# The second product of the stick-breaking scores over 128 rows instead of 64

## The chip, the cores and the metric

The kernel runs on one core of a Trainium2 chip. What counts is the device time of one execution in microseconds (us). It is taken as the median of several runs; one further execution was recorded by the hardware profiler, and all rows below come from that one.

## What is computed

A trunk of two layers over 512 tokens of width 1024, in float32. In each layer three kinds of attention work on the same normalised input, and their results are projected, gated and summed; a SwiGLU feed-forward part (FFN) follows. The change is in the third kind, the stick-breaking attention with 8 heads of 64 features. Its scores are plain products of queries and keys:

```python
def stick_breaking_attention(q, k, v):
    scale = q.shape[-1] ** -0.5
    ...
        z = jnp.einsum('bhqd,bhkd->bhqk', qb, k, preferred_element_type=jnp.float32) * scale
        log_beta = jax.nn.log_sigmoid(z)
        log_keep = jnp.where(mask, jax.nn.log_sigmoid(-z), 0.0)
        suffix = lax.cumsum(log_keep, axis=3, reverse=True) - log_keep
        a = jnp.where(mask, jnp.exp(log_beta + suffix), 0.0)
        return jnp.einsum('bhqk,bhkd->bhqd', a.astype(v.dtype), v)
```

## The kernel before

**Products in two parts.** TensorE is used with operands in the format fp32r. To keep the accuracy of float32, an operand is held as a hi part (rounded to fp32r) and a lo part (what the rounding left). A product of weights and activations is then three products, hi·hi, hi·lo and lo·hi (`mm3`, L199 to L201). The tiles are 128 partitions by 512 columns, one column for each token.

**Order of the work.** TensorE issues in exactly the order in which the program is written; the other engines follow an order that a scheduler makes at build time. Each layer's attention runs in windows 1 to 12, one for each pair of heads: four pairs of forgetting attention (tiles `sf`), four of latent attention (`sm`), four of stick-breaking (`ss`, windows 9 to 12, heads 16 to 23). Within a window the steps of large products (`proj`, `gate`, `o`, three matmuls to a step) stand between the small products of the current head and of the head before it. `SLOTS["s"]` gives that order for a stick-breaking head: the scores of query block 3, then 2, 1, 0, with transposes (L457, `pts`) and products with the values (L468 to L471) of the head before in between.

**The scores of a stick-breaking head.** A pair of heads shares a projection tile: rows 0 to 63 are the first head's features, rows 64 to 127 the second's. `head_q` writes for each head a tile `qa` with the queries' hi in its own 64 rows and their lo in the other 64. `head_k` writes `ka` with the keys' hi in both halves (ScalarE writes one half, L614; a DMA from the GpSimd queue copies it to the other, L616) and the keys' lo (VectorE, L615). So one product over 128 rows (L735) gives hi·hi + lo·hi, and a second one (L736) must add hi(q)·lo(k). Before the change the keys' lo of both heads share one tile `kb`, each head in its own half, and L736 runs over that half alone: 64 rows. For query block i both products have (i + 1)·128 columns, so the widths 512, 384, 256 and 128 occur once for each head. After the scores VectorE adds the mask to the last 128 columns (L423), ScalarE makes two sigmoids (`lefts` and `ps`, L101), VectorE scans and multiplies (L433, L434), and the next head's slot transposes the result.

The forgetting heads have the same pair of products: L675 over 128 rows, and L676 over 66 rows, since two further rows with sums of the gates stand below the keys' lo.

**Rooms.** PSUM tiles of the large products (`mm`) have three buffers; `proj` of a pair's keys stays in one until L615 has read it. The tile `vt` (L399) carries a pair's values from PSUM to their transposes (L404); it has one buffer. `rope_queries` (L696 to L706) makes the rotated queries of four latent heads with VectorE and GpSimd in a tile `qr`. In L199, L735 and so on, L is the line of the kernel before; the changed kernel's lines lie four further on from L734 of it (L739 and L740 are the two products there).

Of the kernel before, what the change touches and what calls it, by code (L numbers as in the profile page):

```python
# [17 lines left out]
P = 128  # L18
D = 1024
S = 512  # L20
# [12 lines left out]
# columns of the constants  # L33
C_INV, C_SGN, C_N = 0, 1, 2
# columns of the small vectors of a layer
# [4 lines left out]
# the blocks of queries whose weights ScalarE normalises  # L40
SCALE_ACT = {"f": (3,), "m": (2, 3)}
# between steps of the products: scores of a head (c), and transposes and products of the head before (p)
# [8 lines left out]
# products of constants that keep TensorE's clock up at the start  # L51
WARM = (24, 12)
# steps of products before each norm of the latents
WAIT = (8, 3, 8, 4)
# the chunk after which the rope tables are made
ROPE_AT = 4
# the chunk of the first products of the FFN after which the second half's norm comes
SS_AT = 3
# how far the work of attention goes before other work in the schedule, and steps by which the weights' division waits
HP, LAG = 30, 1  # L60

# 2*pi in parts of 8 bits, so that a product with a whole number below 2**16 is exact
# [4 lines left out]
def tile_hybrid_trunk(ctx: ExitStack, tc: tile.TileContext, xT, cvec, pos, cst, cmask, vec, gfin,  # L67
# [19 lines left out]
    # TensorE issues in the order written here; the other engines as the scheduler finds best  # L87
    ctx.enter_context(tc.manual_schedule(engines={pe.engine}))

    # ScalarE's functions, in phases of one table set each  # L90
# [15 lines left out]
    def windows(l):  # L106
        """Units of matrix products to run beside the attention of a pair of heads."""
        fox = [[("proj", l, 3 * p + i) for i in range(3)] for p in range(4)]
        sb = [[("proj", l, 12 + 3 * p + i) for i in range(3)] for p in range(4)]
        mla = [[("uqr", l, p // 2)] * (p % 2 == 0) + [("uq", l, p), ("ukv", l, p)] for p in range(4)]  # L110
        mg = [("merge", l, b, m) for b in range(3) for m in range(KC)]
        w = fox + [mla[0], mla[1] + [sb[0][0]], mla[2] + [sb[0][1]], mla[3] + [sb[1][0]], [sb[0][2], sb[1][1]]]
        w.append([mg[0], sb[1][2], mg[1], mg[2]])
        for p in range(2, 4):
            w.append([u for i in range(3) for u in (mg[3 * p - 3 + i], sb[p][i])])
        return w + [mg[9:14], mg[14:16], mg[16:]]
# [42 lines left out]
    def divide(want, after=None):  # L159
        """hi and lo of the weights before the want-th; after: what goes before them on ScalarE and VectorE"""  # L160
        while len(splits) < min(want, len(LOADS)):
            j = len(splits)
            fetch(j + 1)
            c = LOADS[j][2]
            p_, tag = wp, ""
            if fourth[0]:
                fourth[1] += 1
                if fourth[1] % 4 == 1:
                    p_, tag = fourth[0], "x"
            wh = p_.tile([P, D], F32R, tag="wh" + tag, name="wh")  # L170
            ins = [act.copy(wh[:, :c], raws[j][:, :c]).ins]  # L171
            wl = p_.tile([P, D], F32R, tag="wl" + tag, name="wl")
            ins.append(dve.tensor_sub(wl[:, :c], raws[j][:, :c], wh[:, :c].bitcast(F32)).ins)  # L173
            for i, a in zip(ins, after or ()):
                tc.add_manual_dep(i, a.name, order, reason="more urgent")
            splits.append((wh, wl))

    def W(unit, n=1, raw=3, ready=2, lag=0):
        """The next n weights, of that unit on, as (hi, lo); later ones are on their way."""
        i = at[0]  # L180
        if fourth[0]:
            raw, ready = 4, 3
        assert LOADS[i][0] == unit, (LOADS[i][0], unit)
        at[0] = i + n
        divide(i + n)

        def ahead():
            divide(i + max(n, ready + 1))
            fetch(i + max(n, raw + 1))

        if lag:
            later(lag, ahead)
        else:
            ahead()
        return splits[i] if n == 1 else splits[i : i + n]

# [6 lines left out]
    def gemm(o, wt, acts, m=P, start=True, stop=True, c0=0, cols=FULL):  # L203
        """o += W^T a over the chunks of acts, in steps; wt = (hi, lo) holds them m columns each from c0 on."""
        wh, wl = wt
        n = len(acts)
        for k, (ah, al) in enumerate(acts):
            cs = slice(c0 + k * m, c0 + (k + 1) * m)
            mm3(o, wh[:, cs], wl[:, cs], ah[:, cols], al[:, cols], start and k == 0, stop and k == n - 1)
            if k < n - 1:  # L210
                yield
# [12 lines left out]
    def steps(n):  # L224
        """n steps of the products in the queue"""
# [24 lines left out]
    H = S // 2  # L250

    class Norm:
        """1/sqrt(mean of squares over the features) of half the tokens, in every partition."""
# [77 lines left out]
    make_identity(nc, identf)  # L331
    # additive masks of the diagonal block: a query sees keys <= it, and keys < it
# [9 lines left out]
    # rope tables, rows alike in each 32: cos, and -sin | +sin  # L342
# [9 lines left out]
    # sin: +-r; cos: sin(pi/2 - |r|)  # L352
# [10 lines left out]
    def ada(l, i, c, wt=None, on_pool=False, after=None):  # L363
        """Column c of part i of the modulation."""
# [12 lines left out]
        if i in (1, 4):  # L377
            # g * (1 + scale)
# [16 lines left out]
    # ================= layers =================  # L395
    def values(ap, psv, name, got):
        """[2 heads' features, tokens] in PSUM -> [keys, block, head, hi | lo of the features]."""
# [14 lines left out]
    class Head:  # L412
# [4 lines left out]
        def S(self, i):  # L417
# [8 lines left out]
            if self.kind == "s":  # L426
                # sigmoid(z) of the key times the product of sigmoid(-z) over the later keys
# [20 lines left out]
        def T(self, js):  # L448
            """The weights of key blocks js, keys on the partitions, as hi and lo."""
# [12 lines left out]
        def PV(self, j):  # L462
            """[64 features, queries] += values^T weights^T; rows 0-63: hi of the values, rows 64-127: lo."""
# [12 lines left out]
    def slot(cur, prev, n):  # L476
        """The scores of a head and the rest of the head before it, between n steps of the queue."""
# [13 lines left out]
    for l in range(L):  # L491
# [32 lines left out]
        if l == 0:  # L524
# [4 lines left out]
            def warm(n):  # L529
                """Products of constants while there is nothing else: TensorE's clock falls when it idles."""  # L530
# [5 lines left out]
            # room that has no other use yet  # L536
# [65 lines left out]
        # of a head: qa = its queries' hi and lo, ka = its keys' hi twice; kb = its keys' lo  # L602
# [80 lines left out]
        def latent_keys(pr):  # L683
            """The rows that are alike in all heads"""
# [11 lines left out]
        def rope_queries(quad, ts):  # L696
            qr = rp.tile([P, S], F32, tag="qr", name="qr")
# [26 lines left out]
        def stick_tiles(pr, i, t):  # L724
            ts = sbt[pr % 2]
            qa, ka, kb = ts[0:2], ts[2:4], ts[4]
            if i == 0:
                head_q(qa, t)
            elif i == 1:
                head_k(ka, (kb, kb), t, False)  # L730
                vals["s", pr] = []
                for a in range(2):
                    def scores(t, i, n, qa=qa[a], ka=ka[a], kb=kb, me=slice(a * 64, a * 64 + 64)):
                        qs_ = slice(i * P, (i + 1) * P)  # L734
                        pe.matmul(t[:, :n], qa[:, qs_], ka[:, :n], start=True, stop=False)  # L735
                        pe.matmul(t[:, :n], qa[me, qs_], kb[me, :n], start=False, stop=True)  # L736
# [5 lines left out]
        def merge(u, b, m):  # L742
            """merged[m] += sigmoid(gate) * (y_b w_o)"""
# [32 lines left out]
        # the first pair's projections, with the forget gates and the norms of the latents  # L776
        enqueue(0)
        steps(1)
        with scoped(f"fg{l}", "right") as lp:
            # log of the forget gates: min(z, 0) - ln(1 + exp(-|z|)); its sums, negated  # L780
# [31 lines left out]
        sbt = [[sp.tile([P, S], F32R, name=f"sb{j}{i}") for i in range(5)] for j in range(2)]  # L812
# [151 lines left out]
def _inputs(x, c, positions, g_mix, w_ada, b_ada, w_in, b_fox_f, g_mla_q, w_mla_uq, g_mla_kv,  # L964
            w_mla_ukv, w_o_fox, w_o_mla, w_o_sb, w_out, g_ffn, w_ffn_gate, w_ffn_up, w_ffn_down, g_final):
    """The arrays of the launch: the inputs, laid out for it."""
# [5 lines left out]
    def tiles(w):  # L972
        # [L, K, N] -> [L, N / 128, 128 rows of a chunk, chunks, 128]
        l, k, n = w.shape
        return w.reshape(l, k // P, P, n // P, P).transpose(0, 3, 2, 1, 4)
# [4 lines left out]
    def col(v):  # L980
        # [L, n * 128] -> [128, L, n]
# [6 lines left out]
    def qkv(w):  # L988
        # q, k, v tiles of a pair of heads, pair after pair
# [9 lines left out]
    # l kc p quad head part 32 -> l quad p part kc head 32  # L999
    uqr = uqr.reshape(L, 3, P, 2, 4, 2, 32).transpose(0, 3, 2, 5, 1, 4, 6).reshape(L, 2, P, 768)  # L1000
    ukv = np.asarray(w_mla_ukv).reshape(L, 2, P, 4, 2, 2, 64)  # l kc p pair head k|v 64
    ukv = ukv.transpose(0, 3, 2, 5, 1, 4, 6).reshape(L, 4, P, 512)

    wo = np.stack([np.asarray(w_o_fox), np.asarray(w_o_mla), np.asarray(w_o_sb)], axis=1)  # L 3 512 1024
# [15 lines left out]
    # row i: queries of the first half of block i; keys of its second half  # L1020
# [25 lines left out]
# 10000 ** (-i / 16) in float32  # L1046
# [25 lines left out]
```

## Time and profile before

| | |
|---|---|
| runs | 1897.41, 1897.56, 1901.94 us; median 1897.56 us |
| profiled execution | span of 1895.3 us from its first to its last instruction |
| TensorE (PE) | busy 1857.2 us, 98% of the span, 8956 matmuls |
| weight loads (PEld) | busy 1515.1 us, 80%, beside the matmuls |
| VectorE (DVE) | busy 1169.2 us, 62% |
| ScalarE (ACT) | busy 852.1 us, 45% |
| GpSimd (POOL) | busy 141.8 us, 7% |
| granted TensorE clock | 0.995 of full speed, mean over the span |

The profiled execution has no other time on record than its span; the median of the runs is 2.3 us above it. A matmul is two instructions in the trace: a load of the stationary operand (PEld, LDWEIGHTS) and the product that streams the moving operand (PE, MATMUL). Matmuls are pipelined: a record goes on until the result has come out, so records overlap, and the cost of one is read from start to start, not from its duration. "Idle before" with "issue" is time in which an engine waited for nothing that the profile shows.

### The profile page before, as it was taken

The page shows a single profiled execution, that of the slowest core. Times are in us where ns is not written, and L with a number is a line of the kernel's source. Part 1 is how long each engine was busy: PE and PEld are TensorE (multiplying, and loading weights), DVE is VectorE, ACT ScalarE, POOL GpSimd, SP SyncE. Part 2 cuts the span into 40 slices and gives each one's busy share as a digit, 9 for nine tenths or more (in the row PEclk, how much of TensorE's full clock was granted, in tenths as well). Part 3 has the DMA queues.
Part 4 walks back from the last instruction along what each step waited for, and adds up shares of the span by engine and source line. Part 5 has one row for each costly group of instructions (what it writes and reads, how often), then busy time and mean ns, then how long its engine had stood idle before and what let it go on. Part 6 is the DMA issues. An engine that isn't in the chain of part 4 may idle for free.

```text
span 1895.3 us, 24083 instructions
## 1 busy us (share of the span) xinstructions
PE 1857.2 (98%) x8956; PEld 1515.1 (80%) x8956; DVE 1169.2 (62%) x2043; ACT 852.1 (45%) x1543; POOL 141.8 (7%) x260
## 2 busy tenths in 40 slices
PE   6999999999999999999999999999999999999998
PEld 4788787777889888778897887777788888888887
DVE  8888887677756655554558898666664463333333
ACT  4767874443334322232237688544433342232321
POOL 4122100001000000000002121000110000000000
PEclk8999999999999999999999999999999999999999
DMA  7423323333642655555633222122142222223231
GB/s 276 141 73 81 82 79 117 102 110 131 208 150 70 211 177 184 171 184 194 197 107 101 66 68 85 66 84 83 68 145 99 97 100 100 95 95 98 92 92 53
DMA packets 76741, 224.22 MB, mean 118 GB/s; under 512 B 10768, under 2 KB 13968, under 8 KB 76624
## 3 DMA queue, kind: packets, MB, share of 16 engines
q1 hardware_dynamic: 69136, 213.30, 33.8%
q0 software_dynamic: 7488, 9.38, 2.5%
q8 instruction: 71, 1.16, 0.3%
q14 instruction: 46, 0.38, 0.1%
HBM read 209.20 MB, written 4.19 MB: 113 GB/s over the span
## 4 chain that ended last, share of the span: by engine, by line
PE 79%; DMA 9%; DVE 7%; issue 3%; ACT 2%; SPq 0%; DVEq 0%; POOL 0%; POOLq 0%
DMA wraw<-in_w_ada_dram 8%; PE gate L199 5%; PE gate L201 5%; PE gate L200 5%; PE proj L199 4%; PE proj L200 4%; PE dn L200 4%; PE dn L199 4%; PE dn L201 4%; PE proj L201 4%; PE o L199 3%; PE o L200 2%; PE o L201 2%; PE fu L200 2%; PE fu L199 2%
## 5 line engine op out<-in xcount | busy, mean ns | idle before, releaser
L171 ACT CAST wh<-wraw 128x1024 fp32r<-128x1024 f32 (+4 forms) x332 | 311.4, 939 | 560.3 <-PE fu L200 125.1
L173 DVE TENSOR_TENSOR wl<-wraw,wh 128x1024 fp32r<-128x1024 f32 (+4 forms) x332 | 375.8, 1132 | 230.0 <-ACT wh L171 224.7
L372 DVE CUSTOM_DVE_ANT_0 wraw<-wraw,condb 128x1024 f32<-128x1024 f32 x80 | 98.6, 1232 | 153.0 <-DMA wraw<-in_w_ada_dram 152.9
L199 PE MATMUL proj<-uh,wh 128*128 128x512 f32 x384 | 162.2, 422 | 0.0
L199 PE MATMUL gate<-uh,wh 128*128 128x512 f32 x384 | 157.8, 411 | 0.0
L201 PE MATMUL proj<-uh,wl 128*128 128x512 f32 x384 | 151.3, 394 | 0.0
L200 PE MATMUL proj<-ul,wh 128*128 128x512 f32 x384 | 151.3, 394 | 0.0
L201 PE MATMUL gate<-uh,wl 128*128 128x512 f32 x384 | 150.6, 392 | 0.0
L200 PE MATMUL gate<-ul,wh 128*128 128x512 f32 x384 | 150.6, 392 | 0.0
L199 PE MATMUL dn<-hh,wh 128*128 128x512 f32 (+1 forms) x396 | 145.5, 367 | 0.0
L200 PE MATMUL dn<-hl,wh 128*128 128x512 f32 (+1 forms) x396 | 145.4, 367 | 0.0
L201 PE MATMUL dn<-hh,wl 128*128 128x512 f32 (+1 forms) x396 | 144.4, 365 | 0.1
L201 PE MATMUL fu<-uh,wl 128*128 128x512 f32 x336 | 131.5, 391 | 1.6 <-DVE wl L173 1.6
L200 PE MATMUL fu<-ul,wh 128*128 128x512 f32 x336 | 131.0, 390 | 0.0
L199 PE MATMUL fu<-uh,wh 128*128 128x512 f32 x336 | 130.9, 389 | 0.0
L199 PE MATMUL fg<-uh,wh 128*128 128x512 f32 x320 | 125.5, 392 | 0.0
L200 PE MATMUL fg<-ul,wh 128*128 128x512 f32 x320 | 125.5, 392 | 0.0
L201 PE MATMUL fg<-uh,wl 128*128 128x512 f32 x320 | 125.5, 392 | 0.0
L199 PEld LDWEIGHTS gate<-uh,wh 128*128 128x128 f32 x384 | 72.0, 188 | 19.8 <-issue 4.8
L201 PEld LDWEIGHTS proj<-uh,wl 128*128 128x128 f32 x384 | 72.3, 188 | 16.9
L201 PEld LDWEIGHTS gate<-uh,wl 128*128 128x128 f32 x384 | 72.0, 188 | 16.7
L201 PEld LDWEIGHTS dn<-hh,wl 128*128 128x128 f32 x396 | 74.4, 188 | 13.3 <-DVE wl L173 0.5
(370 smaller groups left out, 3973.2 us busy)
## 6 DMA issues: line engine op xcount, KB each, us to landing
wraw<-in_w_proj_dram SPq DMA_DIRECT2D x96, 512.0 KB, 3.5
wraw<-in_w_gu_dram SPq DMA_DIRECT2D x88, 512.0 KB, 3.6
wraw<-in_w_ada_dram SPq DMA_DIRECT2D x80, 512.0 KB, 3.3
wraw<-in_w_dn_dram SPq DMA_DIRECT2D x32, 512.0 KB, 4.0
wraw<-in_w_o_dram SPq DMA_DIRECT2D x48, 256.0 KB, 2.6
wada<-in_w_ada_dram SPq DMA_DIRECT2D x16, 512.0 KB, 5.6
wraw<-in_w_out_dram SPq DMA_DIRECT2D x16, 512.0 KB, 3.5
wraw<-in_w_dn_dram SPq DMA_DIRECT2D x16, 384.0 KB, 3.1
```

Of the source, the lines that this page charges most:

```text
L171: ins = [act.copy(wh[:, :c], raws[j][:, :c]).ins]
L173: ins.append(dve.tensor_sub(wl[:, :c], raws[j][:, :c], wh[:, :c].bitcast(F32)).ins)
L199: pe.matmul(o, wh, ah, start=start, stop=False)
L200: pe.matmul(o, wh, al, start=False, stop=False)
L201: pe.matmul(o, wl, ah, start=False, stop=stop)
L372: ins = dve.tensor_tensor_reduce(out=wt, in0=wt, in1=condb, op0=ALU.mult, op1=ALU.add, scale=1.0, scalar=0.0, accum_out=m).ins
```

## The change

Each stick-breaking head gets a `kb` tile of its own, with its keys' lo in its own 64 rows and zeros in the other 64, and the second product runs over all 128 rows. The zeros are written anew by GpSimd for each tile; the tiles come from a ring of three buffers for the two of a pair. The scores' other operands are as before. To make room, the tile `qr` of the latent queries moves into the one buffer of `vt`.

```diff
         def rope_queries(quad, ts):
-            qr = rp.tile([P, S], F32, tag="qr", name="qr")
+            qr = ap.tile([P, S], F32, tag="vt", name="qr")
...
         def stick_tiles(pr, i, t):
             ts = sbt[pr % 2]
-            qa, ka, kb = ts[0:2], ts[2:4], ts[4]
+            qa, ka = ts[0:2], ts[2:4]
             if i == 0:
                 head_q(qa, t)
             elif i == 1:
-                head_k(ka, (kb, kb), t, False)
+                kb = [sp.tile([P, S], F32R, tag="kb", bufs=3, name=f"kb{a}") for a in range(2)]
+                for a in range(2):
+                    pool.memset(kb[a][64 - a * 64 : 128 - a * 64].bitcast(F32), 0.0)
+                head_k(ka, kb, t, False)
                 vals["s", pr] = []
                 for a in range(2):
-                    def scores(t, i, n, qa=qa[a], ka=ka[a], kb=kb, me=slice(a * 64, a * 64 + 64)):
+                    def scores(t, i, n, qa=qa[a], ka=ka[a], kb=kb[a]):
                         qs_ = slice(i * P, (i + 1) * P)
                         pe.matmul(t[:, :n], qa[:, qs_], ka[:, :n], start=True, stop=False)
-                        pe.matmul(t[:, :n], qa[me, qs_], kb[me, :n], start=False, stop=True)
+                        pe.matmul(t[:, :n], qa[:, qs_], kb[:, :n], start=False, stop=True)
...
-        sbt = [[sp.tile([P, S], F32R, name=f"sb{j}{i}") for i in range(5)] for j in range(2)]
+        sbt = [[sp.tile([P, S], F32R, name=f"sb{j}{i}") for i in range(4)] for j in range(2)]
```

TensorE's order is the same, row for row, but for the operand of the second product. VectorE, ScalarE and GpSimd get new orders, chiefly in window 9 of each layer.

The first place is VectorE in window 9 of the first layer, in which heads 16 and 17 (pair 0) are scored and the key tiles of pair 1 are made. `ss` are scores with the mask added, `lefts` and `ps` the sigmoids, `pl` the lo of transposed weights, `wl` the lo of the large products' weights. Before, the lo of pair 1's second head (`sb_834<-proj,sb_833`) stands early in the window, ahead of the scores of query block 2:

```order
L244 TENSOR_TENSOR yl<-y_166,yh 128x512
L434 TENSOR_TENSOR ps_3041<-ps_3041,lefts_3042 128x512
L615 TENSOR_TENSOR sb_834<-proj,sb_833 64x512
L244 TENSOR_TENSOR plm_3079<-ptm_3077,phm_3078 128x512
L423 TENSOR_TENSOR ss_3092<-ss_3092,mstrict 128x128
L173 TENSOR_TENSOR wl<-wraw,wh 128x1024
```

In the changed kernel it stands (`kb_3008<-proj,sb_832`) right ahead of the mask of query block 0 of head 16 (`ss_3198`):

```order
L173 TENSOR_TENSOR wl<-wraw,wh 128x512
L244 TENSOR_TENSOR plm_3171<-ptm_3169,phm_3170 128x384
L615 TENSOR_TENSOR kb_3008<-proj,sb_832 64x512
L423 TENSOR_TENSOR ss_3198<-ss_3198,mstrict 128x128
L372 ISA wraw,mod_80<-wraw,condb 128x1024
L372 ISA mod_80 128x1
L433 SCALAR_TENSOR_TENSOR lefts_3203<-lefts_3203,onesf 128x128
```

It moved by three query blocks, because the ring has three buffers and this is its fourth tile: `kb_3008` lies where head 16's `kb` lay, and may be written once head 16's last scores are done. A step of the modulation (`mod_80`, L372) now stands between that mask and its scan.

The second place is GpSimd's queue in the same window, from the copy of pair 0's key hi on (`sb_827`). `lefts` are single columns of ones. Before:

```order
L431 MEMSET lefts_3042 128x1
L616 DMA sb_827<-sb_827 64x512
L616 DMA sb_828<-sb_828 64x512
L616 DMA sb_832<-sb_832 64x512
L431 MEMSET lefts_3097 128x1
L616 DMA sb_833<-sb_833 64x512
L431 MEMSET lefts_3146 128x1
L431 MEMSET lefts_3197 128x1
L431 MEMSET lefts_3249 128x1
```

In the changed kernel:

```order
L431 MEMSET lefts_3048 128x1
L616 DMA sb_827<-sb_827 64x512
L616 DMA sb_828<-sb_828 64x512
L616 DMA sb_831<-sb_831 64x512
L431 MEMSET lefts_3103 128x1
L616 DMA sb_832<-sb_832 64x512
L431 MEMSET lefts_3152 128x1
L431 MEMSET lefts_3203 128x1
L733 MEMSET kb_3008 64x512
L431 MEMSET lefts_3255 128x1
```

One clearing of 64 by 512 has come in, behind the ones of head 16's last block. Three others of the layer stand far ahead, among the first pair's key copies of the forgetting attention, and four more among the `lefts` of the later windows.

## Rows read from the trace of the kernel before

**Rows 1.** The page's first line.

```profile
span 1895.3 us, 24083 instructions
```

**Rows 2.** Busy time of each engine in the stick-breaking windows of both layers.

```profile
265.80:457.00 191.20, 190.67 (x862) 146.67 (x860) 140.02 (x233) 88.04 (x164) 13.09 (x42) 1.00 0.34 110
1191.80:1384.00 192.20, 191.67 (x866) 147.40 (x865) 126.14 (x193) 88.38 (x165) 12.96 (x42) 1.00 0.23 76
```

**Rows 3.** Weight loads by line and shape: busy us, mean ns | idle before, releaser.

```profile
L676 PEld LDWEIGHTS sf<-t,t 66*128 66x128 f32 x64 | 12.0, 188 | 2.5
...
L736 PEld LDWEIGHTS ss<-sb,sb 64*128 64x128 f32 x64 | 11.7, 183 | 17.1 <-issue 17.1
```

**Rows 4.** Timeline, head 16, query block 3: start us, duration us, engine.

```profile
266.07 0.40 PE L735 MATMUL ss<-sb,sb 128*128 128x512 f32 x1
...
266.39 0.18 PEld L736 LDWEIGHTS ss<-sb,sb 64*128 64x128 f32 x1 [0.37 <-issue]
...
267.15 0.39 PE L200 MATMUL gate<-ul,wh 128*128 128x512 f32 x1
```

**Rows 5.** TensorE's timeline, head 16, query blocks 2, 1 and 0.

```profile
270.15 0.33 PE L735 MATMUL ss<-sb,sb 128*128 128x384 f32 x1
...
271.11 0.40 PE L200 MATMUL gate<-ul,wh 128*128 128x512 f32 x1
...
275.83 0.28 PE L735 MATMUL ss<-sb,sb 128*128 128x256 f32 x1
...
276.69 0.39 PE L200 MATMUL o<-yl,wh 128*128 128x512 f32 x1
...
281.31 0.22 PE L735 MATMUL ss<-sb,sb 128*128 128x128 f32 x1
...
282.05 0.39 PE L200 MATMUL proj<-ul,wh 128*128 128x512 f32 x1
```

**Rows 6.** TensorE's timeline, a forgetting head, query blocks 3 to 0.

```profile
126.21 0.39 PE L675 MATMUL sf<-t,t 128*128 128x512 f32 x1
...
126.91 0.40 PE L200 MATMUL proj<-ul,wh 128*128 128x512 f32 x1
...
128.51 0.34 PE L675 MATMUL sf<-t,t 128*128 128x384 f32 x1
...
129.10 0.39 PE L200 MATMUL proj<-ul,wh 128*128 128x512 f32 x1
...
131.73 0.28 PE L675 MATMUL sf<-t,t 128*128 128x256 f32 x1
...
132.20 0.40 PE L200 MATMUL proj<-ul,wh 128*128 128x512 f32 x1
...
134.74 0.22 PE L675 MATMUL sf<-t,t 128*128 128x128 f32 x1
...
135.19 0.39 PE L200 MATMUL proj<-ul,wh 128*128 128x512 f32 x1
```

**Rows 7.** GpSimd's clearings of two rows, by line and shape.

```profile
L663 POOL MEMSET t<- 2x512 f32 x8 | 4.0, 519 | 487.4 <-PE dn L201 473.3 <-DVE lat L805 14.0
```

**Rows 8.** Timeline, window 9 of the first layer, VectorE and TensorE.

```profile
271.59 0.69 DVE L615 TENSOR_TENSOR sb<-proj,sb 64x512 fp32r<-64x512 f32 x1
...
281.82 0.30 DVE L423 TENSOR_TENSOR ss<-ss,mstrict 128x128 f32<-128x128 f32 x1 [1.15 <-PE ss L736]
...
284.01 1.23 DVE L372 CUSTOM_DVE_ANT_0 wraw<-wraw,condb 128x1024 f32<-128x1024 f32 x1 [0.61 <-DMA wraw<-in_w_ada_dram]
...
287.11 0.66 PE L404 MATMUL vTs<-identf,vts 128*128 128x128 f32 x4 [0.53 <-ACT vts L399]
...
289.85 0.60 PE L457 MATMUL pts<-identf,ps 128*128 128x128 f32 x4
```

**Rows 9.** Timeline, window 4: GpSimd's last use of `qr`, and the next `vt`.

```profile
174.33 1.29 POOL L705 TENSOR_TENSOR qs<-qr,rh 128x512 fp32r<-128x512 f32 x1 [0.73 <-ACT rh L704]
...
181.47 0.59 ACT L399 COPY vtm<-tv 128x512 f32<-128x512 f32 x1
```

## The prediction

> **What bounds the kernel now.** I began with the page: the span [rows 1], and in the front's table TensorE busy for 98% of it. Such a share is an average over stages, so I then asked for the two stretches in which the changed products stand, windows 9 to 12 of either layer [rows 2]. The reader should compare the first two figures of each row: TensorE's records cover 190.67 of 191.20 us and 191.67 of 192.20 us, at the full granted clock, while VectorE is busy for 140.02 and 126.14 us, ScalarE for 88 and GpSimd for 13. What TensorE spends there is what the stage costs. A share of 99.7% doesn't say that this time is well spent, since records overlap and a product that starts late looks as busy as one that doesn't. For that I read the weight loads by line. The 64 loads of L736 stood idle 17.1 us in all before they began, all put down to "issue", that is, to nothing the profile can name; the 64 loads of L676, the same product of the forgetting heads over 66 rows, stood idle 2.5 us [rows 3]. So a load over 64 rows comes late, one over 66 doesn't.
>
> Then the timeline, to turn this into time. For query block 3 of head 16, L735 starts at 266.07 and the load of L736 only at 266.39, and the second product behind the pair (L200) at 267.15 [rows 4]. I take this stretch, from the start of the pair's first product to the start of the second large product behind the pair, since the load after L736 is late as well and its delay belongs to the cost.
>
> **The change, part by part.**
>
> *The second product over 128 rows.* The stretch for the widths 512, 384, 256 and 128 is 267.15 - 266.07 = 1.08 us [rows 4], and 271.11 - 270.15 = 0.96, 276.69 - 275.83 = 0.86, 282.05 - 281.31 = 0.74 us [rows 5]. The same stretch in a forgetting head, with the same widths, the same products behind, and 128 and 66 rows, is 126.91 - 126.21 = 0.70, 129.10 - 128.51 = 0.59, 132.20 - 131.73 = 0.47 and 135.19 - 134.74 = 0.45 us [rows 6]. The excess is 0.38, 0.37, 0.39 and 0.29 us: nearly the same at all widths, so it is a price for each product and not for its columns. Each width occurs 8 heads by 2 layers = 16 times, and in all 64 cases L199 and L200 follow. The sum is 16 x (0.38 + 0.37 + 0.39 + 0.29) = 16 x 1.43 = 22.9 us. The trace of before shows no stick-breaking product over 128 rows of this kind, so the bounds: below, nothing, if the late load has another cause than the 64 rows; above, 64 times the largest excess, 64 x 0.39 = 25.0 us. I take 22.9, since the forgetting heads are the nearest rows there are, with the same position in the order and the same three large products around. The product itself costs no more over 128 rows than over 66, as L675 and L676 of one pair fit into one stretch of 0.70 us with L199 [rows 6].
>
> *The clearing of the other half.* 16 clearings of 64 x 512 on GpSimd. The nearest row is a clearing of 2 x 512, 0.519 us [rows 7]; I take that, 16 x 0.52 = 8.3 us, on an engine that is busy 13 of 191 us here [rows 2]. Three of each layer are made in the forgetting stage and five between the single-column `lefts`, always behind the ones of the head that frees the buffer, so nothing that is due waits behind a blocked one. Cost: nothing, hidden by GpSimd's idle time.
>
> *The ring of three.* The keys' lo of pair 1's second head (a subtraction of 0.69 us) stood early in window 9; now it waits for head 16's last scores. Behind it on VectorE stand that block's mask, a step of the modulation, and then the scan that the mask feeds. The mask waited for the very same product already, 1.15 us [rows 8], so VectorE loses no work; the mask comes 0.7 us later. The modulation's weights land at about 284.0, and its multiplication takes 1.23 us [rows 8], so the scan starts at about 285.3 instead of right after the mask. TensorE asks for the result at the transposes `pts`, at 289.85 before [rows 8], and by then at most 4 x 0.36 = 1.4 us earlier, 288.4. Some 2 to 3 us of cover remain. In the later windows the buffer's last head has been done for a window when the new keys come. The second thing that is late is the PSUM tile of the keys' projection, held until the subtraction is done, at about 282.5. The next that could need it are the transposes `vTs` at 287.11, which wait 0.53 us for ScalarE's copy anyway [rows 8]. Cover: over 3 us. Cost: nothing.
>
> *`qr` in the room of `vt`.* The copy of the next values must wait until GpSimd has read `qr`: it has at 174.33 + 1.29 = 175.6, and the copy comes at 181.47 [rows 9]. Cover of 5.8 us. Cost: nothing.
>
> *The sum.* 1895.3 - 22.9 = 1872.4 us for the span; the runs' median lies 2.3 us over the profiled span, so 1874.7 us. Behind both stages TensorE goes on as the bound, so what it gains is not waited away later; the stage gets 11.5 us shorter in each layer and VectorE's share there rises to 140.02 / 179.7 = 78%, ScalarE's to 49%.
>
> **The rivals.**
>
> *The gain comes, but new waits take part of it.* A clearing that stands on the path costs 0.52 us; if all 16 did, 8.3 us would go back and the time be 1883.0. Against it: GpSimd's 13 busy us, and the order, in which no clearing stands ahead of something due. The rest of this case is VectorE's queue in window 9, where the cover of 2 to 3 us could be smaller than I read it. 12 in 100.
>
> *The change doesn't do what it says.* If the load of L736 is late for another reason than its 64 rows (that it reads the same queries' tile as the load ahead of it, say), the 0.36 us stay and the time is 1897.6. Against it: the load behind L736 is late as well, and L676 differs in little else. For it: the tile of L676 is another than that of L675, while L735 and L736 read one tile. 5 in 100.
>
> *Slower: the load can't go ahead any more.* A load over all 128 rows might have to wait until the product ahead of it has left the array, while one over 64 rows need not. The second product would then start after L735's record, 266.07 + 0.40, and a load of 0.19 us, at 266.66 instead of 266.39 [rows 4]: 0.27 us, 64 times, 17 us, or 1914.8 us. It decides if the load of the second product begins more than 0.32 us behind the start of the first at 512 columns. The rows speak clearly against it: three products of 512 columns with loads over 66 and 128 rows fit into 0.70 us in the forgetting heads [rows 6], which leaves no room for loads of 0.19 us between them, and it is the 64-row load that stands idle [rows 3]. 2 in 100. The Trainium skill has this as a rule (TensorE: Matmul & The Clock Gate, "Part 3: Packing small matmuls — row/col tiling"): a load overlaps a product in flight only when it goes to another group of rows. By that rule this change would lose the overlap that the second head's 64 rows have; this case's rows show the opposite.
>
> **How the numbers follow.** The forecast, the gain with every cover holding, has 79 in 100, and its own range is 1872 to 1878 us. Part given back: 12, with times up to 1888. No change: 5. Slower: 2. A gain beyond 25.0 us: 2, for waits that shrink along with it. A difference within 0.3% of the time, 5.7 us, can't be told from none here. So faster is 79 + 12 + 2 = 93 in 100, same 5, slower 2. The range begins at 1871, just past the upper bound of the gain (1895.3 - 25.0 + 2.3 = 1872.6), and ends at 1883, where all clearings stand on the path; that leaves out the larger losses, no change and slower, and holds over 8 in 10.
>
> **What would show it.** Right: the idle time "issue" ahead of the second product's loads falls from 17.1 us to about the 2.5 of L676; the four stretches measure 0.70, 0.59, 0.47 and 0.45 us; both stages are about 11.5 us shorter, with TensorE still busy throughout; GpSimd shows 16 clearings of about 0.5 us, and the subtraction of pair 1's second head starts right at the end of head 16's last scores. Wrong: "issue" ahead of those loads stays (the rows aren't the cause); or TensorE shows waits for `ps`, `vTs` or GpSimd in window 9 that it didn't have; or the load of the second product begins only after the first product's record; or the stages shrink and a later one grows by as much.

## The result, and the profile after

The changed kernel takes 1874.53 us (median of 4 runs, 1872.04 to 1876.46), the kernel before beside it 1898.82 us (4 runs, 1897.41 to 1901.94). The ratio is 0.9871, 95% interval 0.986 to 0.9883: faster by 1.3%. The forecast was 1874.7 us. One of e4's four executions below, the profiled one, took 3710.49 us with every product at about half the rate, so its time is that of the other three, and e7 repeats it.

The page's first lines, to be read beside [rows 1] and the front's table:

```profile
span 1872.9 us, 24119 instructions
...
PE 1834.8 (98%) x8956; PEld 1515.9 (81%) x8956; DVE 1167.9 (62%) x2043; ACT 850.4 (45%) x1543; POOL 148.7 (8%) x276
```

TensorE has as many matmuls as before and is still busy for 98%, but the span is 22.4 us shorter. A busy share told nothing of this gain, before or after.

Busy time of each engine over the stick-breaking windows of the changed kernel, beside [rows 2] (columns: stretch, its length, PE, PEld, DVE, ACT, POOL, granted clock, DMA share, GB/s):

```profile
264.20:444.20 180.00, 179.46 (x864) 146.98 (x863) 139.27 (x233) 87.38 (x165) 15.41 (x47) 1.00 0.38 117
1181.10:1361.20 180.10, 179.57 (x865) 147.12 (x864) 124.88 (x192) 87.83 (x165) 15.42 (x47) 1.00 0.26 81
```

TensorE fills these windows as it did, all but 0.5 us, with VectorE at 77% of the first. The weight loads by line and shape, beside [rows 3]:

```profile
L739 PEld LDWEIGHTS ss<-sb,sb 128*128 128x128 f32 x64 | 12.0, 188 | 2.7
...
L740 PEld LDWEIGHTS ss<-kb,sb 128*128 128x128 f32 x64 | 12.0, 188 | 2.5
```

The 17.1 us of "issue" ahead of the second product's loads are gone, and 2.5 us of idle are left. The same place as [rows 4] in the timeline of the changed kernel, head 16, query block 3:

```profile
264.60 0.39 PE L739 MATMUL ss<-sb,sb 128*128 128x512 f32 x1
264.60 0.19 PEld L740 LDWEIGHTS ss<-kb,sb 128*128 128x128 f32 x1
264.83 0.40 PE L740 MATMUL ss<-kb,sb 128*128 128x512 f32 x1
264.83 0.19 PEld L199 LDWEIGHTS gate<-uh,wh 128*128 128x128 f32 x1
265.06 0.39 PE L199 MATMUL gate<-uh,wh 128*128 128x512 f32 x1
265.07 0.19 PEld L200 LDWEIGHTS gate<-ul,wh 128*128 128x128 f32 x1
265.30 0.40 PE L200 MATMUL gate<-ul,wh 128*128 128x512 f32 x1
```

The reader should compare when the load of L740 begins: with the product ahead of it (264.60), not 0.32 us behind as L736's did. Each load runs beside the product ahead, and products follow every 0.23 us. From L739 to L200 it is 0.70 us, where it was 1.08.

**Where the time came from.** Over all 64 pairs, the means of that stretch (16 for each width, read from the timeline of each kernel) went from 1.094, 0.967, 0.855 and 0.742 us to 0.700, 0.579, 0.468 and 0.455 us: 58.5 against 35.2 us in all, a gain of 23.3. The time from the start of a layer's first second product (L736, then L740) to the start of its last went from 190.73 to 179.27 us and from 190.72 to 179.22 us, 23.0 us in all. These four rows of TensorE bound the two in the kernel before:

```profile
266.39 0.50 PE L736 MATMUL ss<-sb,sb 64*128 64x512 f32 x1
...
457.12 0.32 PE L736 MATMUL ss<-sb,sb 64*128 64x128 f32 x1
...
1192.40 0.50 PE L736 MATMUL ss<-sb,sb 64*128 64x512 f32 x1
...
1383.12 0.32 PE L736 MATMUL ss<-sb,sb 64*128 64x128 f32 x1
```

And these four in the changed kernel:

```profile
264.83 0.40 PE L740 MATMUL ss<-kb,sb 128*128 128x512 f32 x1
...
444.10 0.27 PE L740 MATMUL ss<-kb,sb 128*128 128x128 f32 x1
...
1181.77 0.40 PE L740 MATMUL ss<-kb,sb 128*128 128x512 f32 x1
...
1360.99 0.27 PE L740 MATMUL ss<-kb,sb 128*128 128x128 f32 x1
```

The remaining stretches of the span differ by -1.6 us ahead of the first, +2.4 between the two, and -0.2 behind the second; with -11.5 twice this is the span's -22.4. The +2.4 can't be put down to the second product's rows: in this part of the span e1 below, with the old products, has 737.8 us, the changed kernel 737.7 and the kernel before 735.3. Nor do the new tiles explain it: e3 below, with the old tiles, has 739.4 us there, and e6, with the new ones, 735.7. So it varies by some 4 us between the profiled executions, and no run shows that the change has a share in it.

### The profile page after: what moved, and what is told of

The parts are those of the page before. It is cut to its first block, busy times and chain, and to the rows that moved or that the text cites. A ratio compares the mean times of both kernels' runs of the same rounds, so it can differ in the third digit from the quotient of the medians.

```text
span 1872.9 us, 24119 instructions
## 1 busy us (share of the span) xinstructions
PE 1834.8 (98%) x8956; PEld 1515.9 (81%) x8956; DVE 1167.9 (62%) x2043; ACT 850.4 (45%) x1543; POOL 148.7 (8%) x276
## 4 chain that ended last, share of the span: by engine, by line
PE 79%; DMA 9%; DVE 7%; issue 3%; ACT 2%; POOL 0%; SPq 0%; DVEq 0%; POOLq 0%
DMA wraw<-in_w_ada_dram 8%; PE gate L199 5%; PE gate L201 5%; PE gate L200 5%; PE proj L199 4%; PE dn L200 4%; PE proj L200 4%; PE dn L199 4%; PE dn L201 4%; PE proj L201 4%; PE o L199 2%; PE o L200 2%; PE o L201 2%; PE fu L200 2%; PE fu L201 2%
## 5 line engine op out<-in xcount | busy, mean ns | idle before, releaser
L372 DVE CUSTOM_DVE_ANT_0 wraw<-wraw,condb 128x1024 f32<-128x1024 f32 x80 | 97.8, 1223 | 159.5 <-DMA wraw<-in_w_ada_dram 159.4
L200 PE MATMUL proj<-ul,wh 128*128 128x512 f32 x384 | 151.0, 393 | 0.0
L200 PE MATMUL gate<-ul,wh 128*128 128x512 f32 x384 | 150.3, 392 | 0.0
L200 PE MATMUL dn<-hl,wh 128*128 128x512 f32 (+1 forms) x396 | 145.4, 367 | 0.0
L200 PE MATMUL fu<-ul,wh 128*128 128x512 f32 x336 | 130.9, 390 | 0.0
L200 PE MATMUL fg<-ul,wh 128*128 128x512 f32 x320 | 125.5, 392 | 0.0
L199 PEld LDWEIGHTS dn<-hh,wh 128*128 128x128 f32 x396 | 74.4, 188 | 13.1
```

The costliest lines, as they stand in the source:

```text
L199: pe.matmul(o, wh, ah, start=start, stop=False)
L200: pe.matmul(o, wh, al, start=False, stop=False)
L372: ins = dve.tensor_tensor_reduce(out=wt, in0=wt, in1=condb, op0=ALU.mult, op1=ALU.add, scale=1.0, scalar=0.0, accum_out=m).ins
```

## The experiments

Each time stands beside runs of the kernel before on the same chip.

**e1: the new tiles with the old product.** Does the gain come from the rows, or from the tile that each head now has, and what do the clearings and the ring cost?

```diff
-def scores(t, i, n, qa=qa[a], ka=ka[a], kb=kb[a]):
+def scores(t, i, n, qa=qa[a], ka=ka[a], kb=kb[a], me=slice(a * 64, a * 64 + 64)):
...
-pe.matmul(t[:, :n], qa[:, qs_], kb[:, :n], start=False, stop=True)
+pe.matmul(t[:, :n], qa[me, qs_], kb[me, :n], start=False, stop=True)
```

> The changed kernel with its separate, half cleared tiles and their ring, but the second product again over the head's own 64 rows. Theory (the price belongs to a product over 64 rows between products over 128): the four stretches go back to 1.09, 0.97, 0.86 and 0.74 us, 'issue' ahead of the second product's loads back to 17 us, and the time to 1897.5 us (within 1.5 of the kernel before), which also says that the tiles, clearings and the ring cost nothing. Rival (the gain came from each head having a tile of its own): 1874.5 us, stretches as in the changed kernel. Rival (the clearings or the ring cost something that the gain covered): above 1900 us.

Measured: 1898.6 us beside 1898.48, ratio 0.9998 (0.9989 to 1.0007). Mean stretches 1.095, 0.964, 0.855 and 0.744 us. The weight loads of e1:

```profile
L740 PEld LDWEIGHTS ss<-kb,sb 64*128 64x128 f32 x64 | 11.7, 183 | 17.1 <-issue 17.1
```

All of the gain is undone by the rows alone, and what else the change brings (16 clearings, the ring of three, the moved subtraction, `qr` in the room of `vt`) costs nothing that can be measured: the upper end of the interval is 1.3 us. In e1 TensorE leaves the other engines more time than in the changed kernel. For the changed kernel itself the time from a layer's first second product to its last says it: both together shrank by 23.0 of the 23.3 us gained at the 64 pairs.

**e2: 64 rows in another place.** The forgetting heads' second product over 64 rows instead of 66; the sums of the gates are left out of the scores.

```diff
-pe.matmul(t[:, :n], qb[0:66, qs_], kb[0:66, :n], start=False, stop=True)
+pe.matmul(t[:, :n], qb[0:64, qs_], kb[0:64, :n], start=False, stop=True)
```

> The changed kernel with the second product of the forgetting scores over 64 rows instead of 66, so the sums of the gates are left out of the scores. Theory (the row count alone sets the price): 64 more products of 64 rows, stretches 0.70, 0.59, 0.47, 0.45 go to 1.08, 0.96, 0.86, 0.74 us, up to 22.9 us more: 1893 to 1898 us, the lower end if waits of the forgetting stage take some of it in. Rival (the second product was late because it reads the same queries' tile as the first; here it reads another): no change, 1874.5 us.

Measured: 1897.44 us beside 1898.48, ratio 0.9991 (0.9982 to 1.0001). So two rows fewer in 64 products took back what 64 rows more in 64 others had gained. The weight loads of e2, both kinds of heads:

```profile
L740 PEld LDWEIGHTS ss<-kb,sb 128*128 128x128 f32 x64 | 12.0, 188 | 2.5
...
L676 PEld LDWEIGHTS sf<-t,t 64*128 64x128 f32 x64 | 11.7, 183 | 17.2 <-issue 16.4 <-DMA t<-t 0.7
```

Here the two products read different tiles of queries, and the second is late all the same. That rules out the shared tile as the cause.

**e3: twice over 64 rows.** Is it each load over 64 rows that comes late, or the step from 128 rows to 64 and back? In the kernel before, the second product is issued twice, so its term counts twice in the scores.

```diff
-pe.matmul(t[:, :n], qa[me, qs_], kb[me, :n], start=False, stop=True)
+pe.matmul(t[:, :n], qa[me, qs_], kb[me, :n], start=False, stop=False)
+pe.matmul(t[:, :n], qa[me, qs_], kb[me, :n], start=False, stop=True)
```

> The kernel before with the second product issued twice in a row over the same 64 rows, so hi(q) lo(k) is added twice. A plain further product costs its columns, by the changed kernel's stretches 0.23, 0.175, 0.118 and 0.112 us, 16 x 0.635 = 10.2 us. Theory A (the price is for going from 128 rows to 64 and back): the added product pays none of it, 1897.6 + 10.2 = 1907.8 us, its load shows little 'issue'. Theory B (each load over 64 rows comes late, whatever stands ahead of it): the added one pays the late load again, from the start of the first to the start of the second 0.33, 0.26, 0.21 and 0.15 us, 16 x 0.95 = 15.2 us, 1912.8 us, and 'issue' ahead of the loads doubles to some 34 us.

Measured: 1909.62 us beside 1898.48, ratio 1.0059 (1.0044 to 1.0074), 11.1 us more. From the pair's first product to L200 the means are 1.326, 1.139, 0.974 and 0.855 us, 16 times their sum is 68.7 us, 10.2 more than before. In the stretches that is theory A's 10.2 us. The time rose by a little more, 8 to 14 us by the interval, which leaves out theory B's 15.2. The loads of the two second products of e3, by line:

```profile
L737 PEld LDWEIGHTS ss<-sb,sb 64*128 64x128 f32 x64 | 11.9, 186 | 0.0
...
L736 PEld LDWEIGHTS ss<-sb,sb 64*128 64x128 f32 x64 | 11.7, 183 | 17.1 <-issue 17.1
```

The "issue" has not doubled, as theory B had it. The timeline of e3 at head 16, query block 3:

```profile
266.15 0.40 PE L735 MATMUL ss<-sb,sb 128*128 128x512 f32 x1
266.48 0.18 PEld L736 LDWEIGHTS ss<-sb,sb 64*128 64x128 f32 x1 [0.37 <-issue]
266.48 0.50 PE L736 MATMUL ss<-sb,sb 64*128 64x512 f32 x1
266.58 0.19 PEld L737 LDWEIGHTS ss<-sb,sb 64*128 64x128 f32 x1
266.82 0.38 PE L737 MATMUL ss<-sb,sb 64*128 64x512 f32 x1
267.13 0.19 PEld L199 LDWEIGHTS gate<-uh,wh 128*128 128x128 f32 x1 [0.36 <-issue]
```

The added load (L737) waits for nothing: it begins 0.10 us behind the load ahead of it, while that one's product is still streaming. The late loads are the first over 64 rows and the first over 128 behind them. By starts alone the added product looks as late as theory B has it (266.48 to 266.82, 0.34 us), since the record of the product ahead begins with its late load; but the product behind it then follows 0.31 us later (267.13), where 0.43 us passed before. Over the whole stretch the price stands at the two changes.

**e4 and e7: twice over 128 rows.** The same step in the changed kernel, as the measure for e3; e7 is e4 again, for a trace at the usual rate.

```diff
-pe.matmul(t[:, :n], qa[:, qs_], kb[:, :n], start=False, stop=True)
+pe.matmul(t[:, :n], qa[:, qs_], kb[:, :n], start=False, stop=False)
+pe.matmul(t[:, :n], qa[:, qs_], kb[:, :n], start=False, stop=True)
```

> The changed kernel with the second product issued twice in a row over 128 rows, so hi(q) lo(k) is added twice. Both theories: the added product costs its columns alone, 16 x (0.23 + 0.175 + 0.118 + 0.112) = 10.2 us, 1884.7 us, with 'issue' near zero. It is the measure for the same step with 64 rows; and if TensorE didn't bound these windows any more, less than 10.2 us would show.

> The kernel of e4 once more, for a trace at the full granted clock: the second product twice over 128 rows. The added product's load shows no 'issue', and the start of the pair's first product to the second large product behind it is 0.93, 0.755, 0.585 and 0.567 us (0.70, 0.58, 0.468, 0.455 plus 0.23, 0.175, 0.118, 0.112); 1885 to 1886 us.

Measured: e4 1886.20 us (three executions) beside 1898.48, ratio 0.9931 (0.9914 to 0.9947); e7 1884.15 us beside 1899.57, ratio 0.9918 (0.9901 to 0.9935). The stretches of e7 are 0.938, 0.751, 0.582 and 0.569 us, 45.4 us in all, again 10.2 more than without the added product. So an added product costs the same over 64 rows, behind one over the same rows, as over 128, and TensorE is still what these windows wait for: its 10.2 us came out as 11.4 and 8.9 us of time, by the ratios against that of the changed kernel (0.9931 - 0.9871 and 0.9918 - 0.9871 of 1898 us). The two times lie 1.5 us above and 0.9 us below what was expected.

**e5: 32 rows.** The kernel of e1 with only the first 32 of the head's 64 rows; half of the features' lo is left out.

```diff
-def scores(t, i, n, qa=qa[a], ka=ka[a], kb=kb[a], me=slice(a * 64, a * 64 + 64)):
+def scores(t, i, n, qa=qa[a], ka=ka[a], kb=kb[a], me=slice(a * 64, a * 64 + 32)):
```

> The kernel of e1 (separate tiles) with the second product over the first 32 of the head's 64 rows, so hi(q) lo(k) of half the features is left out. Theory (the price is for going from loads over 128 rows to a smaller group of rows and back, whatever its size): stretches and time as with 64 rows, 1.09, 0.97, 0.86, 0.74 us and 1897.5 us. Rival (the price is for the rows that lie idle, or grows with the number of groups): 32 rows cost more than 64, half as much again or double the 0.36 us a pair, 1909 to 1920 us.

Measured: 1899.22 us beside 1899.57, ratio 1.0 (0.9991 to 1.001); stretches 1.091, 0.964, 0.851 and 0.74 us. The weight loads of e5:

```profile
L740 PEld LDWEIGHTS ss<-kb,sb 32*128 32x128 f32 x64 | 11.6, 181 | 17.1 <-issue 17.1
```

The same price as for 64 rows. Between 64 and 32 rows it depends neither on how many rows lie idle nor on the size of the smaller group.

**e6: the keys' lo in both halves.** Instead of zeros a copy of the lo, so the second product adds lo·lo, which the kernel leaves out.

```diff
-                for a in range(2):
-                    pool.memset(kb[a][64 - a * 64 : 128 - a * 64].bitcast(F32), 0.0)
                 head_k(ka, kb, t, False)
+                for a in range(2):
+                    pool.dma_start(out=kb[a][64 - a * 64 : 128 - a * 64], in_=kb[a][a * 64 : a * 64 + 64])
```

> The changed kernel with the keys' lo copied by a DMA to the other half of the tile in place of the zeros, so that the second product adds lo(q) lo(k) as well, which the kernel leaves out. No clearing on GpSimd; 16 DMA issues of 0.51 us in their place. Theory (only the row count matters, zeros cost and save nothing): stretches 0.70, 0.58, 0.47, 0.455 us, 1874.5 us, at most 1 us from it. Rival (rows of zeros stream or load cheaper, or the clearings are cheaper than copies that wait for the subtraction): 1877 us or more, with a wait for a DMA ahead of a head's first second product.

Measured: 1875.46 us beside 1899.57, ratio 0.9878 (0.9863 to 0.9893); stretches 0.703, 0.577, 0.466 and 0.454 us. Its interval and that of the changed kernel overlap. What stands in the added rows makes no difference, and none of these runs points to a faster version: the changed kernel has no product over 64 rows or fewer left.

A product over the head's own half followed by one over the other half, into the same scores, was not run. What a step from one half to the other costs stays open.

## Why the prediction was right

*The second product over 128 rows, 22.9 us.* Right, in mechanism and size. The timelines give 23.3 us for all 64; the four stretches forecast from the forgetting heads (0.70, 0.59, 0.47, 0.45) came out as 0.700, 0.579, 0.468, 0.455. Taking the forgetting heads as the model worked because they differ in what doesn't matter (tiles, two more rows) and agree in what does. The measured excess is 0.39 us at 512, 384 and 256 columns and 0.29 at 128, so it is not quite free of the width. What the prediction left open is how the price is paid. e3 and e5 show it: TensorE pays for leaving the loads over all rows and for coming back, once for each excursion. With 512 columns, the second product begins 0.33 us behind the first instead of 0.24, the one behind it 0.43 us later instead of 0.23, and the next again 0.34 instead of 0.23. The Trainium skill has a rule that would explain this (TensorEngine Tiling (Array Packing), "Key Properties"): a change of tiling mode, and not of the tile alone, drains the engine. The runs agree for rows, with 0.29 to 0.39 us for the way out and back; the drain itself is in no trace.

*The clearing of the other half, nothing.* Right. GpSimd's clearings by line, beside [rows 7]:

```profile
L733 POOL MEMSET kb<- x16: 519/521/554, 81.3 to 1287.6; 64x512 f32 x16
```

16 clearings of 0.52 us (least, median and most are given in ns), the estimate from a clearing of two rows. Rows don't matter there: 64 take as long as the two of [rows 7]. Columns do: a clearing of one column over 128 rows (L431) took 0.10 us.

*The ring of three, nothing.* Right, with less room than elsewhere. VectorE and TensorE of the changed kernel, beside [rows 8]:

```profile
279.00 0.69 DVE L615 TENSOR_TENSOR kb<-proj,sb 64x512 fp32r<-64x512 f32 x1 [0.35 <-PE ss L740]
279.72 0.30 DVE L423 TENSOR_TENSOR ss<-ss,mstrict 128x128 f32<-128x128 f32 x1
281.86 1.23 DVE L372 CUSTOM_DVE_ANT_0 wraw<-wraw,condb 128x1024 f32<-128x1024 f32 x1 [1.84 <-DMA wraw<-in_w_ada_dram]
...
283.01 0.42 DVE L433 TENSOR_TENSOR_SCAN lefts<-lefts,onesf 128x128 f32<-128x128 f32 x1
...
283.57 0.29 DVE L434 TENSOR_TENSOR ps<-ps,lefts 128x128 f32<-128x128 f32 x1
...
284.15 0.66 PE L404 MATMUL vTs<-identf,vts 128*128 128x128 f32 x4 [0.54 <-ACT vts L399]
...
286.50 0.60 PE L457 MATMUL pts<-identf,ps 128*128 128x128 f32 x4
```

The subtraction goes first when the block's last product is done, the mask 0.7 us behind it; then VectorE waits 1.84 us for the modulation's weights, with the scan queued behind. The result is there at 283.86, and TensorE asks for it at 286.50: 2.6 us of cover, where 2 to 3 were forecast. No run had those weights land so much later that TensorE waited. The PSUM tile of the keys' projection is free at 279.69; the transposes `vTs` begin at 284.15 and wait for ScalarE's copy as before, 0.54 us where it was 0.53.

*`qr` in the room of `vt`, nothing.* e1 shows it with the rest. *The sum* was off by 0.2 us, and so close a match is partly luck. The four runs of the changed kernel spread over 4.4 us. The forecast started from 1897.6 us, the before runs beside the result have 1898.8, and by these medians the gain is 24.3 us. That the span lost 22.4 and not the 23.0 us of the windows lies outside them, in differences like the 1.6 and 2.4 us that other executions show too.

*The rivals.* New waits: none of TensorE's waits in these windows grew; its records leave 0.54 and 0.53 us of them uncovered, where it was 0.53 and 0.53. That the change does nothing: e2 takes away its reason. That loads over all rows can't go ahead: the timeline shows L740's load begin with the product ahead, and e7's added loads stood idle 0.7 us in all. The prediction feared there for an overlap that the second head's 64 rows have. There was none to lose: before the change the 64 loads of L736, of both heads, stood idle 17.1 us [rows 3].

## What to carry to other kernels

In this kernel, among products over 128 rows, one over 64 or 32 rows costs 0.39 us more than one over 128 at 256 to 512 columns and 0.29 us more at 128 columns; rows filled with zeros cost nothing. Look for weight loads whose idle time is "issue": the busy share can't show them. If products over few rows are needed, put them next to each other, since the price is paid for each excursion and not for each product. e3 shows this for two products over the same rows with the same operands; other neighbours are open.

## What was not expected of the hardware

Half the columns are not like half the rows. The products with the values run over 128 rows but load only 64 columns of the stationary operand (`128*64`), again between full loads. The weight loads of the changed kernel by line:

```profile
L469 PEld LDWEIGHTS ys<-phs,vs 128*128 128x128 f32 x64 | 12.0, 188 | 5.1
...
L468 PEld LDWEIGHTS ys<-pls,vs 128*64 128x64 f32 x48 | 6.4, 134 | 2.0
```

The loads over 64 columns are shorter, 134 ns instead of 188, and 48 of them stood idle only 2.0 us, none of it "issue". The products keep their pace as well, 0.17 to 0.18 us from start to start at 384 moving columns, into the product over 64 columns' load and out of it:

```profile
297.00 0.34 PE L468 MATMUL ys<-pls,vs 128*64 128x384 f32 x1
297.18 0.33 PE L469 MATMUL ys<-phs,vs 128*128 128x384 f32 x1
297.35 0.39 PE L199 MATMUL gate<-uh,wh 128*128 128x512 f32 x1
```

The Trainium skill's sentence on a change of mode (TensorEngine Tiling (Array Packing), "Key Properties") is not limited to rows; in this case's traces only the rows show a price.

Nor do all row counts below 128 pay. The scores of the latent heads run over 100 and 96 rows, and their loads in the changed kernel show no "issue" either, like those of the forgetting heads over 66:

```profile
L719 PEld LDWEIGHTS sm<-t,t 96*128 96x128 f32 x64 | 12.2, 191 | 0.6
L676 PEld LDWEIGHTS sf<-t,t 66*128 66x128 f32 x64 | 12.2, 191 | 2.6
L718 PEld LDWEIGHTS sm<-t,t 96*128 96x128 f32 x64 | 12.2, 191 | 2.3
...
L717 PEld LDWEIGHTS sm<-t,t 100*128 100x128 f32 x64 | 12.1, 188 | 2.3
```

The kernels have 32 and 64 rows on the dear side and 66, 96, 100 and 128 on the other. Counts between were not run.
